# A hybrid decoder block: transfers that wait for results on GpSimd's queue, gating weights kept on chip, residual rows through shared tiles

## The chip, the cores and the metric

The kernel runs on one core of one Trainium2 chip. The metric is the time of one execution on the device in microseconds, as the median of several runs. The engines are PE (matrix products), DVE (VectorE), ACT (ScalarE), POOL (GpSimd) and SP (SyncE, which computes nothing and issues transfers between the memories). PEld is PE's loading of weights.

## The reference

One layer over 2048 tokens of width 1024. Half of the mixer is attention of eight heads of 64 with three dilated causal windows, merged by their softmax denominators; the other half is a chunked spatial gating unit. A SwiGLU network of width 2816 follows. All inputs and weights are float32.

```python
h = rms_norm(x, pre_mix_norm[l])
proj = h @ w_in[l]                       # q, k, v_a, u, v_s, 512 wide each
q = partial_rotary(q...); k = partial_rotary(k...)
attn = dilated_mixture_attention(q, k, v_a)   # (window, dilation): (128, 1), (512, 4), (2048, 16)
sgu = spatial_gating(u, v_s, ...)        # gelu(u) * (w_spatial @ layer_norm(gelu(v_s)) + b), chunks of 128
mixed = concatenate([rms_norm(attn, ...), rms_norm(sgu, ...)])
x = x + rms_norm(mixed @ w_out[l], post_mix_norm[l])
h = rms_norm(x, pre_ffn_norm[l])
f = (silu(h @ w_gate[l]) * (h @ w_up[l])) @ w_down[l]
x = x + rms_norm(f, post_ffn_norm[l])
```

## The kernel before

The tokens are cut into four blocks `m` of 512. Every float32 operand of a product is split into a high and a low part (`w_hi` and `w_lo`, `hh` and `hl`, `ah` and `al`, `ph` and `pl`), and three matmuls replace one. ACT makes the high part by a copy, DVE the low part by a subtraction.

Results travel through device memory. The projections store q, k and v (`qT`, `kT`, `vD`), the gate stores `sT`, attention stores `aT`, `out_proj` stores the residual `x1`, the feed-forward network stores `fD`. The low parts of `w_in` are stored in `wc` at their first use and read back later (`wcached`); the normalised block 0 is stored in `hD` by `ip_keep` and read back by `ip_again`. Every transfer, load or store, is issued by SP through the method `dma` (L151), so all of them stand in one queue in the order that a scheduler has fixed. An instruction of that queue that waits for a semaphore holds those behind it.

The order of the work, in `build` (L1594 on): the projections of blocks 0 and 1; then, in one merged stream, the attention of blocks 0 and 1 (`tq_heads(0)`) and the rest of the projections and gates (`w1`); then the output projections and the feed-forward network of blocks 0 and 1, merged with the attention of blocks 2 and 3 (`heads(1)`); then the output projections of blocks 2 and 3, `ffn_down(1)`, and the feed-forward network of blocks 2 and 3 with fewer products (`st_up`, `st_down`). `_merge` steps two generators in a given proportion; `R1` and `R2` set the pace of the heads.

`tq_heads` has eight steps ("banks") for each head, four of the far pattern and four of the near one. In each, `tq_scores` computes scores, a maximum and exponentials; two banks later `tq_turn` transposes them; one bank after that `pv` multiplies them with v. The loads of the next head, q, k and v together, are issued in its second bank (L1027). POOL copies q into another order there (L908, tile `q1`). `tq_merge` joins the patterns of two heads: small stores to device memory and loads from it, in three parts that later banks run.

`ip_gate` loads the spatial weights `ws` (1 MB) for each block into a slot of the ring `big` (four slots, L517), which the gate's other tiles and the inputs of the next block share.

`group` (L204) computes four PSUM banks of 128x512 over `nk` steps and calls `evac` for each bank. The projections' `evac` writes tiles of the ring `io` (four buffers) and stores them.

`out_rows` (L1178) ends `out_proj` and `ffn_down`: `evac` writes the tiles `y` (two of them), and after the last bank eight rows of 128x512 are finished by `row`: DVE adds the residual row `xs[i]`, the row is stored, and `fetch` issues the load of a later row. How many rows are loaded ahead is the buffer count of the ring that `ff_pools` names: one buffer `xr` beside `heads(1)`.

The ring `tmp` (four buffers) serves `rbw`, `araw` and `sil`. `high_priority` moves instructions forward in the scheduler's order: scores by 200 (`HP_Q`), transposes by 0 (`HP_T`).

Of the kernel before, what the change touches and what calls it, by code (L numbers as in the profile page):

```python
# [10 lines left out]
F32 = mybir.dt.float32  # L11
# [7 lines left out]
P = 128  # L19
# [64 lines left out]
SU_AT = 1  # L84
XR = 1
T_LAG = 2
T_END = 3
HP_T = 0
BIG = 3.0e38
PV_LAG = 1  # L90
GATE_LAG = 1
PV_BUF = 3
R1 = 1.2
R2 = 1.1
# [18 lines left out]
class Body:  # L113
# [32 lines left out]
    def dma(self, out, in_):  # L146
# [4 lines left out]
        self.nc.sync.dma_start(out, in_)  # L151

    def rstd(self, ss, n, inv_n, eps, name, parts=P):
        v = self.nc.vector
        a = self.tiny.tile([parts, n], F32, name=name + "_a", tag="rs_a", bufs=2, padded_shape=[P, 32])
        y = self.tiny.tile([parts, n], F32, name=name + "_y", tag="rs_y", bufs=5, padded_shape=[P, 32])
        w = self.tiny.tile([parts, n], F32, name=name + "_w", tag="rs_w", bufs=2, padded_shape=[P, 32])
        v.tensor_scalar(a, ss, inv_n, eps, ALU.mult, ALU.add)  # L158
        v.tensor_scalar(y.bitcast(I32), a.bitcast(I32), 1, None, ALU.logical_shift_right)  # L159
        v.tensor_scalar(y.bitcast(I32), y.bitcast(I32), -1, 0x5F3759DF, ALU.mult, ALU.add)  # L160
        for _ in range(3):
            v.scalar_tensor_tensor(w, y, -0.5, y, ALU.mult, ALU.mult)  # L162
            v.tensor_tensor(w, w, a, ALU.mult)  # L163
            v.scalar_tensor_tensor(y, w, 1.5, y, ALU.add, ALU.mult)  # L164
        return y

    def wtile(self, src, perm=False, shape=None, save=None, pool=None, bufs=None):
# [17 lines left out]
        if save is not None:  # L185
            self.dma(save, lo)
        return hi, lo
# [178 lines left out]
    def ip_load2(self, c, pool):  # L366
# [9 lines left out]
        def again(k):  # L376
            self.dma(self.wc[c][k], kept[k][1])
            return kept.pop(k)
# [11 lines left out]
    def ip_keep(self, m):  # L390

        for k in range(KT):
            for i in range(2):
                self.dma(self.hD[k, i], self.h[m][i][k])
                yield

    def ip_again(self, m):

        h = self.ip_tiles(m, self.ip)
        for k in range(KT):  # L400
            for i in range(2):
                self.dma(h[i][k], self.hD[k, i])
            yield
# [27 lines left out]
    def ip_kq(self, m, sec, load, tabs):  # L431
# [3 lines left out]
        def evac(b, ps):  # L435
# [13 lines left out]
            v.tensor_tensor(olv, src, ohv.bitcast(F32), ALU.subtract)  # L449
            self.dma(scr[0][b * P:(b + 1) * P, :], oh)  # L450
            self.dma(scr[1][b * P:(b + 1) * P, :], ol)

        yield from self.group(KT, load, self.feat(m), evac)

    def ip_v(self, m, load):
        nc, pool, v = self.nc, self.ip, self.nc.vector

        def evac(b, ps):
            pv = ps.rearrange("p (h e d) -> p h e d", h=4, e=2)
            for e in range(2):  # L460
                vo = pool.tile([P, 4, 2, HD], F32R, name="io", tag="io", bufs=4)
                nc.scalar.copy(vo[:, :, e, :], pv[:, :, e, :])
                v.tensor_tensor(vo[:, :, 1 - e, :], pv[:, :, e, :], vo[:, :, e, :].bitcast(F32), ALU.subtract)
                self.dma(self.vD[m][e::2, b * P:(b + 1) * P, :].rearrange("h p d -> p h d"),
                         vo.rearrange("p h s d -> p h (s d)"))
# [46 lines left out]
    def ip_gate(self, m):  # L512
# [3 lines left out]
        vh, vl, ug = part["vh"], part["vl"], part["ug"]  # L516
        ws = pool.tile([P, 2, 8, P], F32R, name="ws", tag="big", bufs=4)  # L517
        self.dma(ws, self.wsD)
        for _ in range(GATE_LAG):
# [24 lines left out]
        for ft in range(4):  # L544
# [4 lines left out]
            nc.scalar.activation(o, ps, AF.Copy, scale=self.gT[:, 12 + ft:13 + ft])  # L549
            self.dma(self.sT[m][ft], o)  # L550
            yield
# [73 lines left out]
    def to_row(self, src, dst, name):  # L625

        t = self.tiny.tile([32, 32], F32, name=name + "_w", tag="ln_w", bufs=2)
        self.nc.vector.transpose(t, src)
        self.dma(dst.rearrange("(b a) -> b a", a=32), t)

# [122 lines left out]
    def mix(self, x, h, st, pair):  # L753
# [106 lines left out]
        if h % 2 == 1:  # L860
            for mm in range(2):
# [3 lines left out]
                v.tensor_tensor(t3, t3, rb.rearrange("p (r m i) -> p r m i", r=4, m=2)[:, :, mm, :], ALU.mult)  # L865
                self.dma(self.aT[2 * x + mm][h // 2], at[:, c])
            if h == 1:
# [12 lines left out]

    def tq_pools(self, pool):
        self.ap, self.lt = pool, "at"
        self.tq = pool.tile([P, C_END - C_T4], F32, name="cstq")
        self.dma(self.tq, self.t["consts"][:, C_T4:C_END])

    def tq_load(self, x, h):
# [6 lines left out]

        qs = pool.tile([P, 4, 2, P], F32R, name="qs", tag="qs", bufs=2)
        ql = pool.tile([P, 4, 2, P], F32R, name="ql", tag="ql", bufs=2)
        ks = pool.tile([P, nkm, TB], F32R, name="ks", tag="ks", bufs=2)
# [4 lines left out]
        for m in range(nkm):  # L901
            for s in range(2):
                self.dma(ks[64 * s:64 * s + 64, m, :], rows(self.kT[m][s]))
        q1 = []
        for src in (qs, ql):
            d = pool.tile([P, 8, P], F32R, name="q1", tag="q1", bufs=2)
            for mm in range(2):
                nc.gpsimd.tensor_copy(d[:, 4 * mm:4 * mm + 4, :].rearrange("p j (r i) -> p j r i", r=4),  # L908
                                      src[:, :, mm, :].rearrange("p r (j i) -> p j r i", j=4))
            q1.append(d)  # L910
        v4 = [pool.tile([P, 4, P], F32R, name="v4", tag="v4", bufs=2 * nkm) for _ in range(nkm)]
        n0 = 0 if x == 0 else 7
        v1t = pool.tile([P, 8 * (x + 1) - n0, P], F32R, name="v1", tag="v1", bufs=2)
        for m in range(nkm):
# [3 lines left out]
            if cnt > 0:  # L918
                src = self.vD[m][h].rearrange("(j i r) d -> r i j d", r=4, i=32)
                for r in range(4):  # L920
                    self.dma(v1t[32 * r:32 * r + 32, lo - n0:lo - n0 + cnt, :], src[r, :, 4 - cnt:4])
        return qs, ql, q1, ks, v4, {n: v1t[:, n - n0, :] for n in range(n0, 8 * (x + 1))}

# [10 lines left out]
    def tq_scores(self, x, ld, units, md, h2):  # L934
# [7 lines left out]
        todo = []  # L942
        with self.tc.high_priority(HP_Q):
            for u in units:
# [68 lines left out]
    def tq_heads(self, x):  # L1013
# [6 lines left out]
        def a_step(i):  # L1020
            h, b = divmod(i, nb)
            if b == 0:
                if h == 0:
                    loads[0] = self.tq_load(x, 0)
                if h % 2 == 0:
                    stat[h // 2] = [pool.tile([P, 32], F32, name=n, tag=n, bufs=2) for n in ("tqM", "tqD")]
            if b == 1 and h + 1 < NH:  # L1027
                loads[h + 1] = self.tq_load(x, h + 1)
# [85 lines left out]
    def tq_merge(self, x, pr, stat, outs):  # L1114
# [7 lines left out]
        rr = self.dram.tile([P, 64], F32, name=f"rr{x}_{pr}")  # L1122
        self.dma(rr, T.rearrange("p s i -> p (s i)"))

        C = pool.tile([32, 2, 2, 64], F32, name="tqC", tag="tqC", bufs=1)
        rv = rr.rearrange("(q h t) e -> t q h e", h=2, t=2)
        self.dma(C[:, 1], rv[1])
        rn = rr.rearrange("(q a h t) e -> t a q h e", a=4, h=2, t=2)
        for a in range(4):
            self.dma(C[8 * a:8 * a + 8, 0], rn[0, a])  # L1130
        yield
# [14 lines left out]
        for a in range(4):  # L1146
            self.dma(ww.rearrange("t h (q a i) -> a q (t h) i", a=4, i=32)[a],
                     W[8 * a:8 * a + 8].rearrange("q t h i -> q (t h) i"))
        wb = [pool.tile([P, 4, 2, P], F32, name=n, tag=n, bufs=1) for n in ("ws", "wn")]
        for t in range(2):  # L1150
            for h2 in range(2):
                self.dma(wb[1 - t][64 * h2:64 * h2 + 64].rearrange("p r m i -> p (r m i)"),
                         ww[t, h2].partition_broadcast(64))
# [6 lines left out]
        for mm in range(2):  # L1160
            c = slice(512 * mm, 512 * mm + 512)
            v.tensor_tensor(at[:, c].rearrange("p (i r) -> p r i", r=4), un[:, :, mm, :], a1[:, :, mm, :], ALU.add)
            self.dma(self.aT[2 * x + mm][pr], at[:, c])
        if pr == 0:
# [13 lines left out]
    def out_rows(self, m, n_k, load, ops, res, gain, dst, keep):  # L1178
# [12 lines left out]
        todo = [(n, j) for n in range(2) for j in range(4)]  # L1191
        ahead = self.xr[2]

# [6 lines left out]
        def row(i, r):  # L1200
            n, j = todo[i]
            yj = y[n][:, j, :]
            v.scalar_tensor_tensor(yj, yj, r, xs[i], ALU.mult, ALU.add)
            self.dma(dst[j * P:(j + 1) * P, 512 * n:512 * n + 512], yj)
            if keep:
# [25 lines left out]
    def out_proj(self, m):  # L1231
        nc, t, v, pool = self.nc, self.t, self.nc.vector, self.fp
        ah = [self.fa.tile([P, TB], F32R, name="ah", tag="ah", bufs=KT) for _ in range(KT)]
        al = [self.fa.tile([P, TB], F32R, name="al", tag="al", bufs=KT) for _ in range(KT)]
        rb = pool.tile([P, TB], F32, name="rbw", tag="tmp", bufs=4)
        order = [4, 5, 6, 7, 0, 1, 2, 3]
        with self.tc.high_priority(HP_O):
            for kt in order:
                raw = pool.tile([P, TB], F32, name="araw", tag="tmp", bufs=4)
                if kt < 4:  # L1240
# [29 lines left out]
    def ffn_up(self, m):  # L1270
# [5 lines left out]
        for g in range(NFF // 2):  # L1276
# [17 lines left out]
            def evac(b, ps, g=g, hold=hold):  # L1294
                if b < 2:
                    s = pool.tile([P, TB], F32, name="sil", tag="tmp", bufs=4)
                    nc.scalar.activation(s, ps, AF.Silu)
                    hold[b] = s
                else:
                    s = hold[b - 2]  # L1300
                    v.tensor_tensor(s, ps, s, ALU.mult)
                    ff = 2 * g + b % 2
                    self.dma(self.fD[m][ff], s)

# [9 lines left out]
    def ffn_down(self, m):  # L1314
# [4 lines left out]
        def load_d(k, n):  # L1319
            s = pool.tile([P, TB], F32, name="araw", tag="tmp", bufs=4)  # L1320
            self.dma(s, self.fD[m][k])
# [272 lines left out]
def build(tc, t):  # L1594
    with ExitStack() as ctx:
# [35 lines left out]
        def heads(x):  # L1631
            st, pair = {}, {}
            yield from b.scores(x, 0, st)
            for h in range(NH):
# [6 lines left out]
                for _ in ahead:  # L1641
                    yield
            yield from b.attn_norm(x)

        atx = attn(0, b.tq_pools)
        G = 8 + 2 * GATE_LAG
# [4 lines left out]
                   _merge(b.ip_qkv(3), 30, b.ip_gate(3), 2 * G))  # L1651
        merge(w1, 4 * 50 + 24 + 4 * G, tq_heads(0), 133 * R1)
        atx.close()
# [5 lines left out]
        fa = fax.enter_context(tc.tile_pool(name="fa", bufs=1, side="left"))  # L1659
        b.ff_pools(ff, fa, ff, (ff, "xr", 1))  # L1660
        merge(chain(b.out_proj(0), b.out_proj(1), b.ffn_prep(0), b.ffn_up(0),
                    _merge(b.ffn_down(0), 49, b.ffn_prep(1), 12), b.ffn_up(1)), 269, heads(1), (8 * 29 + 1) * R2)
        atx.close()
        with tc.tile_pool(name="ob", bufs=1, side="right") as ob:
            b.ff_pools(ff, fa, ff, (ob, "xr", 8))
            drain(b.out_proj(2))
            b.ff_pools(ff, ob, ob, (ob, "xr", 8))
            drain(b.out_proj(3))
        fax.close()
        b.hp = ctx.enter_context(tc.tile_pool(name="hp", bufs=1, side="right"))  # L1670
        b.rw = ctx.enter_context(tc.tile_pool(name="rw", bufs=1, side="right"))
        b.ff_pools(ff, None, ff, (ff, "tmp", 4))
        with tc.tile_pool(name="pp", bufs=1, side="right") as pp:
# [37 lines left out]
```

## Time and profile before

| | |
|---|---|
| median of three runs | 2573.8 us (2573.55 to 2574.82) |
| the profiled execution, its own time | 2575.44 us |
| its span, from the first to the last instruction | 2573.7 us |
| mean granted TensorE clock | 0.958 |
| PE busy | 2328.9 us (90% of the span), 10685 matmuls |
| DVE, ACT, POOL busy | 1639.1, 1185.9 and 364.4 us |
| moved by transfers | 479.66 MB, 186 GB/s over the span |
| all of the program's transfers | queue 1, issued by SP |

Busy time counts an engine's own instructions; waiting for semaphores and issuing transfers are not counted. A granted clock of 1 is 2.4 GHz, 0.5 is 1.2 GHz; a mean lies between. A stretch in which PE is busy all the time can still be slow, if its clock is low.

### The profile page before, as it was taken

The page shows a single profiled execution, that of the slowest core. Times are in us where ns is not written, and L with a number is a line of the kernel's source. Part 1 is how long each engine was busy: PE and PEld are TensorE (multiplying, and loading weights), DVE is VectorE, ACT ScalarE, POOL GpSimd, SP SyncE. Part 2 cuts the span into 40 slices and gives each one's busy share as a digit, 9 for nine tenths or more (in the row PEclk, how much of TensorE's full clock was granted, in tenths as well). Part 3 has the DMA queues.
Part 4 walks back from the last instruction along what each step waited for, and adds up shares of the span by engine and source line. Part 5 has one row for each costly group of instructions (what it writes and reads, how often), then busy time and mean ns, then how long its engine had stood idle before and what let it go on. Part 6 is the DMA issues. An engine that isn't in the chain of part 4 may idle for free. (4 is left out here: it accounts for less than half of the span.)

```text
span 2573.7 us, 33168 instructions
## 1 busy us (share of the span) xinstructions
PE 2328.9 (90%) x10685; PEld 1890.1 (73%) x10685; DVE 1639.1 (64%) x3209; ACT 1185.9 (46%) x2278; POOL 364.4 (14%) x338
## 2 busy tenths in 40 slices
PE   7997779989869799999999999998788899999996
PEld 6776667778757678887777887777677688887774
DVE  5524354534569996768899743657677767665566
ACT  6425677556525654535555533545322233334433
POOL 0000000000000000000000000001164567641011
PEclk9998889989989899999999999999999999999998
DMA  7867666776667565456655445776465533326554
GB/s 242 296 193 237 194 201 211 244 215 204 221 207 225 156 214 155 134 154 204 201 163 186 128 123 179 213 221 205 157 214 203 200 111 103 103 86 220 173 193 167
DMA packets 350910, 479.66 MB, mean 186 GB/s; under 512 B 33264, under 2 KB 177168, under 8 KB 350224
## 3 DMA queue, kind: packets, MB, share of 16 engines
q1 hardware_dynamic: 350736, 477.55, 59.1%
q8 instruction: 84, 1.38, 0.2%
q14 instruction: 90, 0.74, 0.1%
HBM read 367.74 MB, written 109.69 MB: 186 GB/s over the span
## 5 line engine op out<-in xcount | busy, mean ns | idle before, releaser
L183 ACT CAST w_hi<-w_raw 128x512 fp32r<-128x512 f32 x368 | 226.7, 618 | 319.7 <-PE d L212 235.0
L184 DVE TENSOR_TENSOR w_lo<-w_raw,w_hi 128x512 fp32r<-128x512 f32 x368 | 255.0, 696 | 183.5 <-ACT w_hi L183 177.3
L212 PE MATMUL d<-ah,w_hi 128*128 128x512 f32 x704 | 275.1, 392 | 1.6 <-ACT ah L338 1.6
L212 PE MATMUL d<-al,w_hi 128*128 128x512 f32 x704 | 275.8, 392 | 0.0
L212 PE MATMUL d<-ah,w_lo 128*128 128x512 f32 x704 | 275.4, 391 | 0.0
L1454 PE MATMUL d<-th,w_lo 128*128 128x512 f32 x616 | 247.3, 402 | 19.5 <-DVE w_lo L1345 19.5
L1454 PE MATMUL d<-th,w_hi 128*128 128x512 f32 x616 | 244.1, 396 | 14.1 <-ACT w_hi L1344 10.1
L1454 PE MATMUL d<-tl,w_hi 128*128 128x512 f32 x616 | 244.4, 397 | 0.0
L1345 DVE TENSOR_TENSOR w_lo<-raw,w_hi 128x512 fp32r<-128x512 f32 x187 | 148.6, 828 | 91.9 <-ACT w_hi L1344 90.9
L1344 ACT CAST w_hi<-raw 128x512 fp32r<-128x512 f32 x187 | 108.4, 618 | 158.3 <-PE d L1536 108.6
L212 PE MATMUL d<-w_hi,hh 128*128 128x512 f32 x384 | 157.2, 412 | 19.6 <-ACT w_hi L201 9.6
L212 PE MATMUL d<-w_lo,hh 128*128 128x512 f32 x384 | 157.1, 409 | 5.5 <-DMA w_lo<-wc 4.9
L212 PE MATMUL d<-w_hi,hl 128*128 128x512 f32 x384 | 154.9, 405 | 0.0
L1454 PEld LDWEIGHTS d<-th,w_lo 128*128 128x128 f32 x616 | 117.9, 191 | 50.3 <-DVE w_lo L1345 25.8
L212 PEld LDWEIGHTS d<-ah,w_hi 128*128 128x128 f32 x704 | 132.1, 188 | 27.1 <-ACT ah L338 1.8
L212 PEld LDWEIGHTS d<-ah,w_lo 128*128 128x128 f32 x704 | 132.3, 188 | 26.0
L212 PEld LDWEIGHTS d<-al,w_hi 128*128 128x128 f32 x704 | 132.3, 188 | 25.7
L212 PE MATMUL d<-w_hi,fl 128*128 128x512 f32 x352 | 139.9, 405 | 11.3 <-DVE fl L1312 11.2
L212 PE MATMUL d<-w_hi,fh 128*128 128x512 f32 x352 | 143.3, 407 | 5.5 <-ACT fh L1311 5.5
L1454 PEld LDWEIGHTS d<-th,w_hi 128*128 128x128 f32 x616 | 117.9, 191 | 40.6 <-ACT w_hi L1344 10.7
L212 PE MATMUL d<-w_lo,fh 128*128 128x512 f32 x352 | 140.6, 400 | 0.0
L1454 PEld LDWEIGHTS d<-tl,w_hi 128*128 128x128 f32 x616 | 118.0, 191 | 27.1
(312 smaller groups left out, 5473.5 us busy)
## 6 DMA issues: line engine op xcount, KB each, us to landing
w_raw<-in_w_in SPq DMA_DIRECT2D x136, 256.0 KB
w_lo<-wc SPq DMA_DIRECT2D x96, 256.0 KB
w_raw<-in_w_gate SPq DMA_DIRECT2D x88, 256.0 KB
w_raw<-in_w_up SPq DMA_DIRECT2D x88, 256.0 KB
w_raw<-in_w_down SPq DMA_DIRECT2D x88, 256.0 KB
araw<-fD SPq DMA_DIRECT2D x88, 256.0 KB
raw<-fS SPq DMA_DIRECT2D x77, 256.0 KB
w_raw<-in_w_out SPq DMA_DIRECT2D x64, 256.0 KB
```

Of the source, the lines that this page charges most:

```text
L183: nc.scalar.copy(hv, rv)
L184: nc.vector.tensor_tensor(lv, rv, hv.bitcast(F32), ALU.subtract)
L212: nc.tensor.matmul(banks[b], lhsT, rhs, start=(k == 0 and j == 0), stop=(k == nk - 1 and j == len(ops) - 1))
L1344: nc.scalar.copy(hv, src)
L1345: nc.vector.tensor_tensor(lv, src, hv.bitcast(F32), ALU.subtract)
L1454: nc.tensor.matmul(ps, a[:, c], b, start=(k == 0 and n == 0), stop=(k == 3 and n == 2))
```

## The change

A method `put` issues a transfer from GpSimd's queue. The stores of results (`wc`, `hD`, `qT`, `kT`, `vD`, `sT`, `aT`, `fD`, the rows of `x1` and of the output in `out_rows`, the small ones of `to_row`), the reads of `hD` and all transfers of `tq_merge` use it. All other loads, and the transfers of `st_up` and `st_down`, stay on SP.

The gating weights `ws` are loaded once, into the pool of the first attention half, and `ip_gate` uses that tile.

`tq_load` loads q and k alone, into one buffer of q instead of two, at the sixth bank of the head before; the new `tq_near` makes the POOL copies and loads v in the first bank of the head itself. The heads of the first half get more steps (1.25 instead of 1.2), transposes get priority 200 and scores 0.

The ring `tmp` has five buffers; beside `heads(1)` the residual rows go through it, three ahead, and `xr` is gone there. In `ffn_down(1)` four of five are ahead.

```diff
-XR = 1
+T_BUF = 5
...
-HP_T = 0
+HP_T = 200
+HP_S = 0
...
-R1 = 1.2
+R0 = 1.25
...
+    def put(self, out, in_):
+        if out.dtype == F32R:
+            out = out.bitcast(F32)
+        if in_.dtype == F32R:
+            in_ = in_.bitcast(F32)
+        self.nc.gpsimd.dma_start(out, in_)
...
-            self.dma(save, lo)
+            self.put(save, lo)
...
-            self.dma(self.wc[c][k], kept[k][1])
+            self.put(self.wc[c][k], kept[k][1])
...
-                self.dma(self.hD[k, i], self.h[m][i][k])
+                self.put(self.hD[k, i], self.h[m][i][k])
...
-                self.dma(h[i][k], self.hD[k, i])
+                self.put(h[i][k], self.hD[k, i])
...
-            self.dma(scr[0][b * P:(b + 1) * P, :], oh)
-            self.dma(scr[1][b * P:(b + 1) * P, :], ol)
+            self.put(scr[0][b * P:(b + 1) * P, :], oh)
+            self.put(scr[1][b * P:(b + 1) * P, :], ol)
...
-                self.dma(self.vD[m][e::2, b * P:(b + 1) * P, :].rearrange("h p d -> p h d"),
+                self.put(self.vD[m][e::2, b * P:(b + 1) * P, :].rearrange("h p d -> p h d"),
...
-        ws = pool.tile([P, 2, 8, P], F32R, name="ws", tag="big", bufs=4)
-        self.dma(ws, self.wsD)
+        ws = self.ws
...
-            self.dma(self.sT[m][ft], o)
+            self.put(self.sT[m][ft], o)
...
-        self.dma(dst.rearrange("(b a) -> b a", a=32), t)
+        self.put(dst.rearrange("(b a) -> b a", a=32), t)
...
-                self.dma(self.aT[2 * x + mm][h // 2], at[:, c])
+                self.put(self.aT[2 * x + mm][h // 2], at[:, c])
...
-    def tq_pools(self, pool):
+    def tq_pools(self, x, pool):
...
+        if x == 0:
+            self.ws = pool.tile([P, 2, 8, P], F32R, name="wgt")
+            self.dma(self.ws, self.wsD)
...
-        qs = pool.tile([P, 4, 2, P], F32R, name="qs", tag="qs", bufs=2)
-        ql = pool.tile([P, 4, 2, P], F32R, name="ql", tag="ql", bufs=2)
+        qs = pool.tile([P, 4, 2, P], F32R, name="qs", tag="qs", bufs=1)
+        ql = pool.tile([P, 4, 2, P], F32R, name="ql", tag="ql", bufs=1)
...
-        q1 = []
-        for src in (qs, ql):
+        return [qs, ql, None, ks, None, None]
+    def tq_near(self, x, h, ld):
+        nc, pool = self.nc, self.ap
+        nkm = 2 * (x + 1)
+        ld[2] = []
+        for src in ld[:2]:
...
-            q1.append(d)
-        v4 = [pool.tile([P, 4, P], F32R, name="v4", tag="v4", bufs=2 * nkm) for _ in range(nkm)]
+            ld[2].append(d)
+        v4 = [pool.tile([P, 4, P], F32R, name="v4", tag="v4", bufs=4) for _ in range(nkm)]
...
-        v1t = pool.tile([P, 8 * (x + 1) - n0, P], F32R, name="v1", tag="v1", bufs=2)
+        v1t = pool.tile([P, 8 * (x + 1) - n0, P], F32R, name="v1", tag="v1", bufs=2 - x)
...
-        return qs, ql, q1, ks, v4, {n: v1t[:, n - n0, :] for n in range(n0, 8 * (x + 1))}
+        ld[4:] = v4, {n: v1t[:, n - n0, :] for n in range(n0, 8 * (x + 1))}
...
-        with self.tc.high_priority(HP_Q):
+        with self.tc.high_priority(HP_S):
...
+                self.tq_near(x, h, loads[h])
...
-            if b == 1 and h + 1 < NH:
+            if b == ns + 1 and h + 1 < NH:
...
-        self.dma(rr, T.rearrange("p s i -> p (s i)"))
+        self.put(rr, T.rearrange("p s i -> p (s i)"))
...
-        self.dma(C[:, 1], rv[1])
+        self.put(C[:, 1], rv[1])
...
-            self.dma(C[8 * a:8 * a + 8, 0], rn[0, a])
+            self.put(C[8 * a:8 * a + 8, 0], rn[0, a])
...
-            self.dma(ww.rearrange("t h (q a i) -> a q (t h) i", a=4, i=32)[a],
+            self.put(ww.rearrange("t h (q a i) -> a q (t h) i", a=4, i=32)[a],
...
-                self.dma(wb[1 - t][64 * h2:64 * h2 + 64].rearrange("p r m i -> p (r m i)"),
+                self.put(wb[1 - t][64 * h2:64 * h2 + 64].rearrange("p r m i -> p (r m i)"),
...
-            self.dma(self.aT[2 * x + mm][pr], at[:, c])
+            self.put(self.aT[2 * x + mm][pr], at[:, c])
...
-        ahead = self.xr[2]
+        ahead = self.xr[3]
...
-            self.dma(dst[j * P:(j + 1) * P, 512 * n:512 * n + 512], yj)
+            self.put(dst[j * P:(j + 1) * P, 512 * n:512 * n + 512], yj)
...
-        rb = pool.tile([P, TB], F32, name="rbw", tag="tmp", bufs=4)
+        rb = pool.tile([P, TB], F32, name="rbw", tag="tmp", bufs=T_BUF)
...
-                raw = pool.tile([P, TB], F32, name="araw", tag="tmp", bufs=4)
+                raw = pool.tile([P, TB], F32, name="araw", tag="tmp", bufs=T_BUF)
...
-                    s = pool.tile([P, TB], F32, name="sil", tag="tmp", bufs=4)
+                    s = pool.tile([P, TB], F32, name="sil", tag="tmp", bufs=T_BUF)
...
-                    self.dma(self.fD[m][ff], s)
+                    self.put(self.fD[m][ff], s)
...
-            s = pool.tile([P, TB], F32, name="araw", tag="tmp", bufs=4)
+            s = pool.tile([P, TB], F32, name="araw", tag="tmp", bufs=T_BUF)
...
-        atx = attn(0, b.tq_pools)
+        atx = attn(0, lambda pool: b.tq_pools(0, pool))
...
-        merge(w1, 4 * 50 + 24 + 4 * G, tq_heads(0), 133 * R1)
+        merge(w1, 4 * 50 + 24 + 4 * G, tq_heads(0), 133 * R0)
...
-        b.ff_pools(ff, fa, ff, (ff, "xr", 1))
+        b.ff_pools(ff, fa, ff, (ff, "tmp", T_BUF, 3))
...
-            b.ff_pools(ff, fa, ff, (ob, "xr", 8))
+            b.ff_pools(ff, fa, ff, (ob, "xr", 8, 8))
...
-            b.ff_pools(ff, ob, ob, (ob, "xr", 8))
+            b.ff_pools(ff, ob, ob, (ob, "xr", 8, 8))
...
-        b.ff_pools(ff, None, ff, (ff, "tmp", 4))
+        b.ff_pools(ff, None, ff, (ff, "tmp", T_BUF, T_BUF - 1))
```

## Rows read from the trace of the kernel before

**Rows 1.** Busy time by stage: stretch, its length, engines (instructions), clock, DMA share, GB/s.
```profile
core 0: us, PE busy (x) PEld busy (x) DVE busy (x) ACT busy (x) POOL busy (x), PEclk, DMA share, GB/s
0.00:186.00 186.00, 166.28 (x736) 132.31 (x736) 80.61 (x169) 87.42 (x168) 2.54 (x9) 0.99 0.75 247
186.00:380.00 194.00, 148.28 (x730) 119.25 (x729) 83.27 (x260) 116.14 (x268) 7.48 (x13) 0.87 0.69 208
380.00:712.00 332.00, 301.90 (x1547) 248.18 (x1546) 165.31 (x439) 199.93 (x439) 11.07 (x16) 0.96 0.70 220
712.00:860.00 148.00, 107.22 (x497) 87.25 (x496) 117.32 (x270) 60.06 (x123) 6.80 (x19) 0.85 0.68 208
860.00:1850.00 990.00, 945.39 (x4412) 774.70 (x4410) 722.24 (x1443) 481.44 (x848) 41.78 (x85) 0.99 0.58 174
1850.00:2574.00 724.00, 659.80 (x2772) 528.46 (x2772) 470.31 (x632) 240.94 (x434) 294.70 (x196) 0.96 0.48 162
```
**Rows 2.** Waits of PE, 186 to 860 us: total, times, longest.
```profile
PE qk L728 <- DMA ks<-kT: 21.8, 4, 12.9
PE d L212 <- DVE y L1212: 14.6, 2, 14.3
PE d L212 <- ACT w_hi L201: 9.6, 1, 9.6
PE qk L527 <- DMA ws<-wsD: 9.1, 1, 9.1
...
PE d L212 <- DVE io L449: 5.9, 4, 1.7
PE d L212 <- DMA w_lo<-wc: 4.9, 1, 4.9
```
**Rows 3.** Waits of SP's queue, 186 to 860 us: total, times, longest.
```profile
SPq L151 <- PE d L212: 86.4, 60, 5.4
SPq L151 <- ACT io L549: 21.2, 12, 6.4
...
SPq L151 <- ACT io L448: 17.3, 10, 5.8
```
**Rows 4.** Timeline of SP, 238 to 249 us: start, length, issue.
```profile
238.65 2.38 SPq L151 DMA_DIRECT2D hh<-hD  x1
...
245.85 0.62 SPq L151 DMA_DIRECT2D w_raw<-in_w_in  x1
```
**Rows 5.** Timeline of SP, 709 to 742 us.
```profile
709.01 1.29 SPq L151 DMA_DIRECT2D qs<-qT  x2
...
715.69 3.10 SPq L151 DMA_DIRECT2D vD<-io  x4
...
721.52 2.63 SPq L151 DMA_DIRECT2D vD<-io  x4
...
740.29 0.32 SPq L151 DMA_DIRECT2D araw<-aT  x1
740.66 1.83 SPq L151 DMA_DIRECT2D ks<-kT  x3
```
**Rows 6.** Instructions on tile y, 760 to 870 us: ns min/median/max, first and last start.
```profile
L1203 DVE SCALAR_TENSOR_TENSOR y<-y,po_y,xr x8: 699/746/753, 811.4 to 848.8; 128x512 f32<-128x512 f32 x8
L151 SPq DMA_DIRECT2D x<-y x8: 320/330/338, 812.1 to 849.6; - x8
```
**Rows 7.** Transfers by issue, whole span: engine, count, size of one.
```profile
fD<-sil SPq DMA_DIRECT2D x44, 256.0 KB
...
rA<-an_w SPq DMA_DIRECT2D x2, 4.0 KB
```
**Rows 8.** Groups of POOL's instructions by form, whole span: busy us, mean ns.
```profile
L1475 POOL TENSOR_TENSOR fs<-fs 128x512 f32<-128x512 f32 x11 | 19.1, 1740 | 0.0
...
L908 POOL CAST q<-qs 128x512 fp32r<-128x512 f32 x16 | 10.4, 677 | 582.6 <-issue 203.9 <-PE qk L964 198.0 <-DMA ql<-qT 179.3
```
**Rows 9.** Timeline of SP, 329 to 342 us.
```profile
336.27 5.49 SPq L151 DMA_DIRECT2D v<-vD  x8
```
**Rows 10.** The profile's costliest groups: one of the projections' three matmuls, mean ns.
```profile
L212 PE MATMUL d<-w_hi,hh 128*128 128x512 f32 x384 | 157.2, 412 | 19.6 <-ACT w_hi L201 9.6
```

## The prediction

> **What bounds the kernel now.** I read the stage windows first, because a mean over the whole span hides that the stages have different limits. PE is the busiest engine in every stage [rows 1], so time is won where PE sits idle or runs at the lower clock. Up to 186 us and after 1850 us the change touches little or nothing that PE waits for: the last stages issue their transfers as before. From 860 to 1850 us PE is idle for 990 − 945.4 = 44.6 us and its clock is 0.99, so little is to be had there. What is left is 186 to 860 us: (194 − 148.3) + (332 − 301.9) + (148 − 107.2) = 116.6 us idle, at clocks of 0.87, 0.96 and 0.85 [rows 1]. A clock of 0.87 means that a quarter of the stretch ran at 1.2 GHz. If all of these stretches had been busy, the half speed would have cost 0.13 × 194 + 0.04 × 332 + 0.15 × 148 = 61 us; much of it coincides with the idle time itself, so I call it 15 to 35 us. 116.6 + 35, some 150 us, is the ceiling of any gain in this part.
>
> Next, PE's own waits there [rows 2]: a few long ones carry it, and five name data that came late: `ks` (21.8 us in 4), `y` (14.6, of which one is 14.3), `w_hi` at L201 (9.6), `ws` (9.1), `w_lo` from `wc` (4.9). Then SP's waits [rows 3], since SP issues every load. SP is one queue in order: an issue that waits holds all behind it. It waits 86.4 us for PE to free a buffer, and 21.2 + 17.3 = 38.5 us in two rows for results that are only to be stored (`sT`, and the q and k tiles).
>
> Three SP timelines show what stands behind these waits. At 238.65 us a read of `hD` takes 2.38 us, where others take 0.38, because a buffer is not free yet; more reads follow, and only at 245.85 does the `w_raw` load go out [rows 4]; PE's 9.6 us wait for `w_hi` lies there. Between 715.69 and 724.15 us two blocks of `vD` stores sit inside the first head's q and k loads of the second attention half, and later the last `araw` load goes out only at 740.29, when a `tmp` buffer is free, with three `ks` loads behind it [rows 5]. And the eight rows of `out_proj`'s residual run from 812.1 to 849.6 us, 5.36 us apart, though each is one 0.75 us DVE instruction [rows 6]: with one `xr` buffer, load, DVE and store follow one another. PE's 14.3 us wait ends when these rows have given `y` back.
>
> **The change part by part.** *Transfers to GpSimd's queue.* By the issue counts, from `fD` (x44) to `rA` (x2), 358 transfers move [rows 7]. In 186 to 860 us POOL is busy for 7.5 + 11.1 + 6.8 us only [rows 1], so there is room. What an issue costs POOL the trace does not show. Below stands SP's 0.33 us [rows 6], above POOL's dearest instruction, 1.74 us; nearest is its copy of a 128x512 tile, 0.68 us [rows 8], since both handle one tile of that size. I take 0.7: 358 × 0.7 = 251 us spread over 1700, and even 1.74 gives 623. POOL doesn't become the bound as a whole.
>
> What it frees, wait by wait: (a) the `hD` reads leave the `w_raw` load's path, and `ws` is no longer loaded for each gate: 9.6 + 9.1 = 18.7 us of PE waiting [rows 2]. Each head's q, k and v loads stay on SP and still stand before some `w_raw` loads, so I take 12 of 18.7 (ends 0 and 18.7). (b) `w_lo` from `wc`, held up by q stores: 4.9, all of it. (c) `ks`: of 21.8 us the `vD` blocks cost 3.10 + 2.63 us and the waits around them, 8.5 us from the first to the last; a fifth `tmp` buffer lets one more load ahead. I take 9 (ends 0 and 21.8). (d) Elsewhere from 860 to 1850: 3 of 44.6 us.
>
> What is queued behind the new waits: on POOL the copies to `q1` (L908) and `k1` (L590) and the memsets at L831. The k1 copies serve a head that starts later, q1 is needed four score steps after its issue; a bank takes (712 − 186) / 64 = 8 us, so 33 us cover it. Without that cover each of the eight heads would lose a transfer's wait, some 3 us, 24 in all. The `hD` reads also wait on POOL now; behind them stand stores whose tiles have a ring of four.
>
> *That ring is the cost.* `io` has four buffers, a q or k bank takes two, and one comes back when its transfer has landed. PE already waits 5.9 us for it at L449 [rows 2]. Twelve projection groups of eight stores each: at 0.7 instead of 0.33 us a group's last store goes out 8 × 0.37 = 3 us later, 36 us in all if nothing hid it. The attention instructions that are mixed in, and the next group's first three banks, hide most: I take 8 lost (ends 0 and, at 1.74 us, 135).
>
> *Gating weights kept.* The four 1 MB loads become one, ahead of the first head's q loads: at 208 GB/s [rows 1] 1 MB takes 5 us. I take 3 lost there; the gain is in (a).
>
> *Loads of a head.* q and k now go out three score steps before use (24 us) rather than seven, v three steps before its product. Eight v loads took 5.49 us with their waits [rows 9] and two q loads 1.29 [rows 5], so a head's ten and twelve issues take some 7 and 8 us and stay hidden: 0. Cover gone, the first head loses up to 15 us, once.
>
> *Residual rows through three shared tiles.* Three loads in flight instead of one take the row chain from 37.5 us towards eight DVE instructions and one transfer, about 15 us. PE needs it only 14.3 us earlier, so all of that wait goes: 14 (ends 7, if the rows still wait behind other DVE work, and 14.6).
>
> *Priorities and pace* (transposes first, scores later, 1.25 for 1.2): the heads end some nine of 264 steps earlier, leaving nine more without attention to mix in. No row prices it: I take 0, with 10 to either side.
>
> Sum: 12 + 4.9 + 9 + 3 + 14 = 43 gained, 8 + 3 = 11 lost, and of the clock's 15 to 35 us 10 come back, as the longest idle stretches go: 42 net. The profiled execution's span 2573.7 becomes 2532. Its own time, 2575.4, is 1.7 above its span; the median of the runs is 2573.8, so by the same difference I say 2532 for the median. A change within 0.2% (5 us) can't be told from none.
>
> **The rivals.** *Nothing that matters is moved.* If the loads are late because transfers are slow, not because stores stand before them, PE waits stay. DMA shares of 0.69 and 0.70 [rows 1] speak for it, the timelines [rows 4, 5] against. Then only `y`'s 14 us come back and the 11 us of cost eat them: 2571. The Trainium skill has a rule that leads here ("DMA: Bandwidth & Descriptors", section "Issuing engines are not separate DMA queues"): several issuing engines share the same DMA engines and only save the sequencer's issue time; by it the SP time saved is no gain, as SP is not the bound. It doesn't speak of loads held behind a waiting store, which the SP timelines here show.
>
> *GpSimd's queue is slow and `io` sets the pace: slower than before.* At 1.74 us an issue the twelve groups lose 8 × 1.41 = 11.3 us each, 135 in all, and with half hidden by attention work 68. 43 + 10 − 3 gained against 68 lost: 2573.8 + 18 = 2592. It decides from about 1.4 us an issue on (half of 96 × 1.04 is 50). For it speaks that DVE is busy most of the time in 712 to 860 us [rows 1] and its two-input work shares the memory with POOL's; against it, that the next group's 96 matmuls of 0.41 us, 39 us, pass before these buffers are wanted again [rows 10]. The Trainium skill ("SBUF — State Buffer", section "Who interferes with whom") warns of this: a transfer issued by GpSimd needs descriptors that GpSimd writes, and some VectorE modes lock it out meanwhile. No run here shows it.
>
> *More comes back.* If q, k and weight loads all run ahead once SP is free, about two thirds of the 150 us ceiling goes: 2474.
>
> **How the numbers follow.** Likeliest, 2532: 0.60, its own range 2505 to 2558 (terms at their ends). More comes back: 0.16. Nothing moved: 0.08. Slower: 0.16. The range reaches into the rivals on both sides: 2480 to 2590 leaves about 2 in 10. Faster by over 0.2%: 0.60 + 0.16 = 0.76; same 0.08; slower 0.16.
>
> **What would show it.** Right: the waits of PE for `ws` and for `y` around 840 us are gone; the residual rows stand 2 us apart; the clock in 186 to 380 and 712 to 860 us is above 0.9; SP no longer waits for `io`. Wrong: POOL busy over 300 us more, PE waiting for `io` (L449, L463) tens of us, `q1` or `k1` late, or the head's first scores waiting for q, k or v.

## The result: slower by 1.2%

| kernel | median | executions | against before, 95% interval |
|---|---|---|---|
| before | 2574.3 us | 2573.6 to 2576.6 (4) | |
| after | 2606.0 us | 2598.0 to 2611.6 (4) | 1.0119 [1.0091, 1.0147] |

The forecast was 2532 us and faster, its range 2480 to 2590: wrong in sign and outside the range. The profiled execution of after took 2611.6 us, the longest of its four; its span is 2609.9.

Stages of the kernel after, in the stretches of [rows 1] (the last one is longer, as the span is):

```profile
core 0: us, PE busy (x) PEld busy (x) DVE busy (x) ACT busy (x) POOL busy (x), PEclk, DMA share, GB/s
0.00:186.00 186.00, 151.46 (x644) 119.02 (x645) 75.33 (x158) 81.06 (x156) 47.74 (x90) 0.94 0.66 226
186.00:380.00 194.00, 148.17 (x745) 120.90 (x744) 82.00 (x254) 114.37 (x258) 38.79 (x68) 0.88 0.72 213
380.00:712.00 332.00, 297.85 (x1535) 246.19 (x1536) 154.93 (x424) 204.86 (x454) 63.55 (x110) 0.94 0.65 197
712.00:860.00 148.00, 114.42 (x495) 91.06 (x494) 108.78 (x241) 59.84 (x114) 21.53 (x41) 0.87 0.73 236
860.00:1850.00 990.00, 937.65 (x4353) 769.07 (x4351) 724.50 (x1468) 476.97 (x836) 88.96 (x179) 0.97 0.57 173
```

The first stage, which the forecast left out, lost most: PE 151.5 us busy for 166.3, 644 matmuls for 736, clock 0.94 for 0.99. The stretch that was to win has the same busy time as before (148.2) and nearly the same clock (0.88 for 0.87). Followed by the starts of the same matmuls in both traces: the 65th of `d<-w_hi,hh` comes at 192.7 us for 171.2 (21.5 late); the first of `d<-ah,w_hi` at 896.6 for 879.1 (17.5); the 65th of those at 983.6 for 942.3 (41.3). The rest keeps that distance, 36 us at the end.

PE's waits of after, 186 to 860 us (total, times, longest), beside [rows 2]:

```profile
PE qk L736 <- DMA ks<-kT: 14.5, 5, 6.9
PE d L221 <- DVE io L458: 13.9, 7, 6.2
PE qk L535 <- DVE pl L1027: 11.3, 2, 11.2
PE d L221 <- ACT w_hi L192: 8.9, 2, 6.3
...
PE d L221 <- DVE io L472: 6.5, 2, 6.0
```

`ws` is gone, `y` is gone from this list, `ks` is 7 us less. But `io` takes 20.4 us (13.9 + 6.5) where it took 5.9. SP's queue in the same stretch, beside [rows 3], and the rows of `out_proj`, beside [rows 6]:

```profile
SPq L152 <- PE d L221: 220.8, 78, 49.5
SPq L152 <- ACT w_hi L210: 29.2, 33, 6.2
```

```profile
L1221 DVE SCALAR_TENSOR_TENSOR y<-y,po_y,xr x8: 734/746/752, 832.7 to 841.0; 128x512 f32<-128x512 f32 x8
L160 POOL DMA_DIRECT2D x<-y x8: 540/541/555, 835.7 to 842.0; - x8
```

SP waits no more for the engines that fill `io` (9.6 us for `vD` stores to land before v is loaded remain); it stands 220.8 us at PE's free buffers for 86.4, so loads run as far ahead as their buffers allow. The rows are 1.2 us apart for 5.36. Both came as forecast, and the kernel got slower.

Groups of POOL by form: busy us, mean ns. An issue costs 0.54 us, one of 512-byte rows (`vD`) 0.755; POOL is busy 201 us more, 565.7 in all.

```profile
L160 POOL DMA_DIRECT2D vD<-io x32 | 24.1, 755 | 73.6 <-DVE io L472 70.2 <-issue 1.7 <-DVE tqM L986 0.8
L160 POOL DMA_DIRECT2D fD<-sil x44 | 23.9, 542 | 275.4 <-DVE sil L1319 260.9 <-DVE S L754 12.5 <-PE pv L817 1.9
```

### The profile page after: what moved, and what is told of

Read it like the earlier page. It is cut to its first block, busy times and chain, and to the rows that moved or that the text cites. A ratio compares the mean times of both kernels' runs of the same rounds, so it can differ in the third digit from the quotient of the medians.

```text
span 2609.9 us, 33572 instructions
## 1 busy us (share of the span) xinstructions
PE 2342.9 (90%) x10685; PEld 1901.3 (73%) x10685; DVE 1641.8 (63%) x3209; ACT 1196.2 (46%) x2288; POOL 565.7 (22%) x696
## 5 line engine op out<-in xcount | busy, mean ns | idle before, releaser
L221 PE MATMUL d<-w_hi,hh 128*128 128x512 f32 x384 | 157.8, 413 | 28.1 <-DVE io L458 12.9
```

Source lines behind the costliest of these rows:

```text
L221: nc.tensor.matmul(banks[b], lhsT, rhs, start=(k == 0 and j == 0), stop=(k == nk - 1 and j == len(ops) - 1))
```

## The experiments

Each runs against the kernel before on the same chip; "us against before" is (ratio − 1) × 2574. A difference between two runs carries both intervals: some 10 us against e2, whose interval is the widest, 6 to 9 between most others.

### The moves against the other parts

e1 is the changed kernel with the first moved stores back on SP (first diff), e2 with all of them (second diff), e4 with the old priorities and pace (third). e3 is the kernel before with `put` in place of `dma` at the 18 places of the change, and nothing else.

```diff
-            self.put(save, lo)
+            self.dma(save, lo)
...
-            self.put(self.wc[c][k], kept[k][1])
+            self.dma(self.wc[c][k], kept[k][1])
...
-                self.put(self.hD[k, i], self.h[m][i][k])
+                self.dma(self.hD[k, i], self.h[m][i][k])
```

```diff
-        self.nc.gpsimd.dma_start(out, in_)
+        self.nc.sync.dma_start(out, in_)
```

```diff
-HP_T = 200
-HP_S = 0
+HP_T = 0
+HP_S = 200
...
-R0 = 1.25
+R0 = 1.2
```

> The changed kernel, with the stores of wc and hD back on SP's queue. Theory (early stores): on GpSimd's queue these stores leave as soon as their tiles are ready, from 19 us on, and take the transfer engines from the loads of w_raw, so ACT's copies and the normalisation behind them come late. Then PE's 7.8 us gap at 38.7 us and the half clock after it are gone, the work that stands at 193 us in the changed kernel stands near 172 us, and the time is about 2606 - 19 = 2587. Rival (order): the first 190 us are late because the other edits made the scheduler order the loads differently; then the gap stays and the time is 2600 to 2612.

> The changed kernel with every moved transfer back on SP's queue; kept gating weights, later loads of a head, pace and residual rows stay as changed. Theory (the move to GpSimd's queue is what costs, 19 us up to 193 us and some 24 us from 880 to 1040 us): the time falls to 2574 less the gains of the other parts (14 for the rows, some 9 for ws): 2550 to 2565. Rival (the loss after 880 us comes from the residual rows or the pace of the heads): only the first 19 us come back and the gains of the move are lost: 2585 to 2605.

> The kernel before with the transfers moved to GpSimd's queue and nothing else. Theory (the move costs): the early stores show as in the changed kernel, +19 us by 193 us, the later waits for w_lo and ks shrink by some 10: 2580 to 2600. Rival (the move is harmless, the other parts cost): 2555 to 2575.

> The changed kernel with the old priorities and pace: scores 200, transposes 0, 1.2 for 1.25. Theory (the move costs): within 8 us of the changed kernel, 2598 to 2612. Rival (priorities and pace upset the merged stream from 186 to 712 us): the stretch shortens by over 10 us, 2580 to 2595.

| run | median | ratio, 95% | us against before |
|---|---|---|---|
| e1 early stores on SP | 2598.7 | 1.0070 [1.0053, 1.0087] | +18 |
| e2 all on SP | 2548.8 | 0.9886 [0.9850, 0.9922] | −29 |
| e3 moves alone | 2617.8 | 1.0147 [1.0122, 1.0171] | +38 |
| e4 old pace | 2611.2 | 1.0110 [1.0089, 1.0132] | +28 |

The move to GpSimd's queue is the loss: without it the rest of the change is 29 us faster than before, 60 us from the changed kernel. e3, the moves alone, lies above the 2580 to 2600 that was expected. Pace and priorities show no part in it (e4: 2 us less than the changed kernel, within 9). The first stores carry less than the theory said, 13 us of its 19 (31 − 18), and little of it where the theory put it: PE's 7.8 us gap at 38.7 us is gone in e1, but others come in its place, and the 65th `d<-w_hi,hh` comes at 188.7 us, only 4 earlier than in the changed kernel. By the order of PE's matmuls e1 is 1 us behind the kernel before when the changed kernel stands at 50 us, and 15 behind when it stands at 150. One wait shows why. Timelines of e1, POOL and ACT:

```profile
49.68 0.73 POOL L160 DMA_DIRECT2D kT<-io  x1 [48.37 <-ACT io L457]
51.41 1.08 POOL L160 DMA_DIRECT2D kT<-io  x2 [1.00 <-DVE io L458]
```

```profile
56.49 1.02 ACT L457 CAST io<-d 128x512 fp32r<-128x512 f32 x1 [4.99 <-DMA kT<-io]
```

and the same wait in the kernel before, whose SP issued that store at 48.46:

```profile
51.44 1.08 ACT L448 CAST io<-d 128x512 fp32r<-128x512 f32 x1 [0.87 <-DMA kT<-io]
```

ACT waits for the first `io` buffer to come back: 6.8 us after its store is issued in e1, 3.0 before. That wait is of the transfer, not of the issue: the store of 49.68 us takes 0.73 us to issue and 6.7 to land.

### Which of the moves

e5 is e1 with the residual rows' stores on SP as well (first diff); e6 the changed kernel with the `io` stores on SP (second). The others go the other way, from e2, with one kind of transfer on GpSimd's queue: e7 the `io` stores (the second diff reversed), e11 the reads of `hD` (third), e12 the stores of the rows (the first reversed).

```diff
-            self.put(dst[j * P:(j + 1) * P, 512 * n:512 * n + 512], yj)
+            self.dma(dst[j * P:(j + 1) * P, 512 * n:512 * n + 512], yj)
```

```diff
-            self.put(scr[0][b * P:(b + 1) * P, :], oh)
-            self.put(scr[1][b * P:(b + 1) * P, :], ol)
+            self.dma(scr[0][b * P:(b + 1) * P, :], oh)
+            self.dma(scr[1][b * P:(b + 1) * P, :], ol)
...
-                self.put(self.vD[m][e::2, b * P:(b + 1) * P, :].rearrange("h p d -> p h d"),
+                self.dma(self.vD[m][e::2, b * P:(b + 1) * P, :].rearrange("h p d -> p h d"),
...
-            self.put(self.sT[m][ft], o)
+            self.dma(self.sT[m][ft], o)
```

```diff
-                self.dma(h[i][k], self.hD[k, i])
+                self.put(h[i][k], self.hD[k, i])
```

> The changed kernel with the stores of wc and hD and the residual rows' stores back on SP. Theory (the loss between 880 and 1040 us comes of the residual rows when their stores leave SP's queue: in the kernel with every transfer on SP it is not there, in the one with the moves alone neither): 22 us of 2598.7 come back, 2574 to 2582, and the work that stands at 942 us in the kernel before is no later against its start at 879 us than there. Rival (that loss follows from something else that was moved, as aT or fD): 2592 to 2602.

> The changed kernel with the stores from the ring io (q, k, v and sT) back on SP; all else as changed. Theory (a tile of the ring comes back later when its store shares the transfer engines with loads that SP no longer holds up; that costs some 25 us from 80 to 720 us): 2578 to 2588, PE's waits for io under 12 us. Rival (the ring costs little, the hD reads and the small stores of the merge do): 2598 to 2610.

> The changed kernel with every transfer on SP but the stores from the ring io, which stay on GpSimd's queue. Theory (ring): 2549 + 25, so 2566 to 2580, and PE waits for io some 20 us. Rival (ring costs little): 2545 to 2556.

> Every transfer on SP but the 16 reads of hD, which go out on GpSimd's queue. Theory of the prediction (these reads stood before the w_raw load that PE waited 9.6 us for): 5 to 10 us less than with all on SP, 2538 to 2545. Rival (the kept gating weights gave that wait back already, and the reads now run beside the w_raw loads): 2547 to 2556.

> Every transfer on SP but the stores of the residual rows (x1 and the rows of the output that out_rows writes), which go out on GpSimd's queue. Theory (these stores leave in bursts and hold up the loads of later rows and of xs; DVE waits for them in order, and the scores behind it): about 20 us more than with all on SP, 2564 to 2574, lost between 850 and 1000 us. Rival (they cost only together with the other moves): 2545 to 2556.

| run | median | ratio, 95% | us against before | against e2 |
|---|---|---|---|---|
| e5 | 2580.1 | 1.0022 [1.0007, 1.0037] | +6 | |
| e6 | 2614.5 | 1.0149 [1.0127, 1.0171] | +38 | |
| e7 `io` moved | 2568.7 | 0.9974 [0.9959, 0.9990] | −7 | +22 |
| e11 `hD` reads moved | 2560.1 | 0.9929 [0.9916, 0.9943] | −18 | +11 |
| e12 rows moved | 2565.3 | 0.9961 [0.9948, 0.9974] | −10 | +19 |

Each of the three kinds costs by itself, 22 + 11 + 19 = 52 of 60 us, each within some 10 us by e2's interval, so that the 11 of the `hD` reads is barely clear of none. (The stores of `wc`, `hD`, `aT` and `fD` and the merge were not tried alone.) The rows' theory holds from both sides: e5 is 12 us faster than e1, a little less than the 16 to 25 expected, and e12's loss lies where it should. Stretch from the first to the 65th `d<-ah,w_hi` in e2, after and e12:

```profile
853.00:917.00 64.00, 61.84 (x313) 50.92 (x314) 58.39 (x145) 39.81 (x74) 2.97 (x9) 0.97 0.69 210
```

```profile
897.00:984.00 87.00, 70.66 (x315) 57.25 (x314) 70.73 (x170) 46.22 (x82) 10.35 (x20) 0.82 0.52 162
```

```profile
855.00:941.00 86.00, 69.98 (x315) 56.64 (x316) 71.80 (x176) 46.93 (x82) 8.51 (x17) 0.86 0.54 165
```

The same 313 to 315 matmuls take 64 us with the stores on SP, 87 and 86 with them moved: some 14 us of idle time more, and the rest is the clock, 0.82 and 0.86 for 0.97. What starts it, in four views of e12: the timelines of SP, POOL and DVE, and PE's waits (total, times, longest).

```profile
869.01 2.25 SPq L152 DMA_DIRECT2D xr<-in_x  x3
871.36 0.86 SPq L152 DMA_DIRECT2D xs<-x  x2
872.31 0.41 SPq L152 DMA_DIRECT2D w_raw<-in_w_gate  x1
```

```profile
869.28 0.54 POOL L160 DMA_DIRECT2D x<-y  x1 [17.68 <-DVE y L1221]
870.54 2.53 POOL L160 DMA_DIRECT2D x<-y  x4 [0.72 <-DVE y L1221]
```

```profile
875.48 0.75 DVE L1221 SCALAR_TENSOR_TENSOR y<-y,po_y,xr 128x512 f32<-128x512 f32 x1 [2.11 <-DMA xr<-in_x]
```

```profile
PE qk L736 <- DVE S L744: 5.1, 1, 5.1
```

Within 4 us SP issues six loads and POOL five stores of 256 KB. The row of the last loads waits 2.11 us on DVE, the next one 0.5, in order; the scores wait behind them, and PE waits 5.1 us for the scores, from 873.4 to 878.6 us. The granted clock falls to 0.5 at 874.9 us, for 6.8 us. In e2 the same stores stand between these loads in SP's queue, and no row of this stretch waits. But the moved stores also changed the order that the scheduler fixed for DVE: in e12 the scores' instruction (L744) stands behind all eight rows, in e2 behind five. The waits for loads are 2.6 of PE's 5.1 us; how much of the stretch's 22 us is the transfers and how much the order was not separated. In e3, with one row at a time, this stretch lost 3 us: the rows three ahead and their moved stores cost only together.

The same reserve holds for every run here: an edit of a transfer makes the scheduler fix another order of the engines' work. PE's order leaves that of e2 at 52 us in e7, at 237 in e11 and at 792 in e12. A run's cost is that of the move together with the order that came with it.

e6 refutes that undoing one kind gives its cost back. In the first stage the kinds don't add: the 65th `d<-w_hi,hh` comes at 188.7 us in e1, 188.8 in e6, 189.1 in e7 and 192.7 in the changed kernel, for 169.7 in e2. Either kind is enough to lose that stage. By the order of PE's matmuls e6 is still 8 us ahead of the changed kernel at 676 us, 3 at 735, and within 2 of it from 780 to 900; between lies 740.6 us, where PE waits 12.4 us for `araw` from `sT` (12.9 in e2; the changed kernel has no such wait). Why that load is late was not followed up.

e11 refutes the forecast's term for the `hD` reads. Issued by POOL they take 6.9 us to land (median), and PE waits 5.9 us for a `w_hi` at 226.9 us; in e2 its longest wait for one from 200 to 260 us is 2.3. The time, 2560, lies above the rival's range too (2547 to 2556).

### A second queue, or GpSimd's?

The same stores from ScalarE's queue, all else as in e7 and e12:

```diff
-        self.nc.gpsimd.dma_start(out, in_)
+        self.nc.scalar.dma_start(out, in_)
```

> As the run before, but the stores from the ring io leave on the queue of ScalarE instead of GpSimd's: again a second queue, but not the one that needs GpSimd. Theory (what costs is that the stores share the engines with SP's loads): about the same, 2560 to 2585, and ACT's own waits for the low parts come on top. Rival (GpSimd's queue itself is slow): tiles come back as fast as from SP (1.7 us) and the time is 2540 to 2556.

> Every transfer on SP but the stores of the residual rows, which go out on ScalarE's queue. Theory (any second queue lets the burst of rows run beside the loads that DVE and PE wait for): near the run with these stores on GpSimd's queue, 2560 to 2572, lost between 850 and 1000 us. Rival (it is GpSimd's queue): as with all on SP, 2543 to 2555.

| run | median | ratio, 95% | us against before | against e2 |
|---|---|---|---|---|
| e8 `io` on ScalarE's queue | 2552.0 | 0.9907 [0.9889, 0.9925] | −24 | +5 |
| e13 rows on ScalarE's queue | 2571.7 | 0.9973 [0.9956, 0.9990] | −7 | +22 |

For the rows it is a second queue, whichever: 22 us against 19. For `io` it isn't: e8 can't be told from e2, and it is 17 us (within 6) faster than e7. Its time lies below the theory's range and in the rival's (2540 to 2556), though the rival's reason, tiles back as fast as from SP, doesn't hold. From issue to a store's last packet, worked out by counting the packets of each queue off against its issues (q, k, v and `sT` stores, 190 to 720 us):

| queue of the `io` stores | least | median |
|---|---|---|
| SP (e2) | 1.6 us | 2.1 us |
| ScalarE (e8) | 1.6 us | 3.1 us |
| GpSimd (e7) | 1.9 us | 3.4 us |

The least times are close; at the median a store takes 1.0 us more on the second queue, and GpSimd's adds 0.3. By the semaphores that tell of the landing the medians are 2.9, 4.2 and 4.4 us. So the tiles come back late on either queue; the first stage loses 10 us in e8 and 19 in e7. PE's wait for `io` up to 720 us in e8, beside those of the next section (the lines of its kernel are shifted by eight):

```profile
PE d L229 <- DVE io L466: 17.2, 9, 5.3
PE d L229 <- DVE io L480: 2.1, 1, 2.1
```

By the order of PE's matmuls e8 is 14 us behind e2 at the 2000th, 11 at the 3000th and 1 at the 3500th, and e7 26, 32 and 22. Some 10 us come back in both where e2 has its 12.9 us wait for `araw`, which they don't have. So late tiles cost time in e8 too while the `io` stores run, and its end hides it. What the other 17 us of e7 are stays open; 0.3 us a store doesn't explain them.

### Is it the ring?

Six `io` buffers for four in every tile of that ring, paid for with a buffer each of `ph` and `pl`; e14 is e7 with it, e15 is e2 with it.

```diff
-PV_BUF = 3
+PV_BUF = 2
...
-            oh = pool.tile([P, TB], F32R, name="io", tag="io", bufs=4)
-            ol = pool.tile([P, TB], F32R, name="io", tag="io", bufs=4)
+            oh = pool.tile([P, TB], F32R, name="io", tag="io", bufs=6)
+            ol = pool.tile([P, TB], F32R, name="io", tag="io", bufs=6)
...
```

> The stores from the ring io on GpSimd's queue, all else on SP, with six buffers in that ring in place of four (and two instead of three of ph and pl, to make room). Theory (late tiles cost time because the ring is short): the 20 us against the kernel with all on SP shrink to 0 to 8, PE's waits for io fall under 12 us. Rival (the loads that the stores delay cost the time): the distance to the run with six buffers and all on SP stays 15 to 25.

> The same six buffers of io and two of ph and pl, with every transfer on SP: the measure for the run before. Theory (ring): 2543 to 2556, PE's waits for io gain little from two more buffers here. Rival: the two buffers of ph and pl cost more than 10 us, 2560 or more, and the run before is to be read against that.

e14: 2559.0 us, 0.9925 [0.9900, 0.9950], −19 us. e15: 2551.6 us, 0.9889 [0.9868, 0.9910], −29 us. With two more buffers the moved `io` stores cost 13 us less (e14 against e7, within 8), and nothing shows with all on SP (e15 against e2, within 11). Their cost falls from 22 to 9 us. PE's wait for `io` (0 to 720 us) in e2, e7, e14, e15:

```profile
PE d L221 <- DVE io L458: 8.5, 8, 2.7
PE d L221 <- DVE io L472: 1.5, 2, 1.3
```

```profile
PE d L221 <- DVE io L458: 22.0, 12, 6.8
PE d L221 <- DVE io L472: 4.9, 3, 3.6
```

```profile
PE d L221 <- DVE io L458: 13.0, 6, 5.3
```

```profile
PE d L221 <- DVE io L458: 7.6, 6, 3.1
```

The wait is 10.0 us in e2 and 26.9 in e7; two more buffers take it to 13.0 in e14, and by the medians more than half of the cost with it: the short ring is what makes late tiles cost time, for that part. The 9 us left are hardly more than the noise.

### The other parts, with all transfers on SP

Both start from e2: e9 puts the residual rows back as before (the diff), e10 the priorities and the pace (the diff of e4).

```diff
-T_BUF = 5
+T_BUF = 4
...
-        b.ff_pools(ff, fa, ff, (ff, "tmp", T_BUF, 3))
+        b.ff_pools(ff, fa, ff, (ff, "xr", 1, 1))
...
-        b.ff_pools(ff, None, ff, (ff, "tmp", T_BUF, T_BUF - 1))
+        b.ff_pools(ff, None, ff, (ff, "tmp", T_BUF, T_BUF))
```

> Every transfer on SP, and the residual rows as in the kernel before (one buffer of their own beside the heads, ring tmp of four); kept gating weights, later loads and pace as changed. Theory of the prediction (the rows give 14 us): 2549 + 14, so 2558 to 2568. Rival (the wait for y goes, but its time is lost again in the same stretch; without the move the stretch from 706 to 853 us is as long as before): 2544 to 2555.

> Every transfer on SP, priorities and pace of the heads as in the kernel before; kept gating weights, later loads and rows as changed. Theory of the prediction (pace is worth nothing, within 10): 2545 to 2558. Rival (of the 25 us that the kernel with all on SP gains, 16 of them from 250 to 365 us, the pace carries most): 2560 to 2575.

e9: 2561.6 us, 0.9938 [0.9926, 0.9949], −16 us: the rows are worth 13 us, within 10. e10: 2541.0 us, 0.9861 [0.9847, 0.9875], −36 us: by the medians the new pace costs 7 where nothing is moved, but within 10, so that it isn't shown. e10 has the lowest median: kept weights, later loads, rows through `tmp`, one queue, old pace. The kept weights and the later loads gain 16 us with the new pace (e9), and some 23 (36 − 13) if the pace's 7 are real; they were not tried apart, since the second q buffers make the room for `ws`.

## Why the prediction was wrong

**"Up to 186 us ... the change touches little or nothing that PE waits for."** The step that failed first. The stage stores `hD`, `wc`, q, k and v, and these moved. In [rows 1] it had a DMA share of 0.75 at 247 GB/s, the highest of all, and loads that PE lives on. By the same count of packets a `w_raw` load issued from 18 to 48 us takes 2.6 us (median of 5) in the kernel before and 6.0 (of 9) after, where 26 stores leave beside them from 19.15 us on. The stretch from 18 to 48 us in before, after and e1 (columns as above):

```profile
18.00:48.00 30.00, 26.98 (x132) 20.88 (x132) 19.82 (x48) 24.37 (x50) 0.00 (x0) 1.00 0.73 249
```

```profile
18.00:48.00 30.00, 21.13 (x100) 16.64 (x101) 16.47 (x42) 22.02 (x48) 14.13 (x26) 0.90 1.02 387
```

```profile
18.00:48.00 30.00, 26.15 (x127) 20.32 (x128) 18.87 (x46) 24.00 (x49) 0.00 (x0) 1.00 0.78 254
```

The DMA engines, at a share of 0.73, are full after the move (1.02), with the stores and with more loads that SP is now free to issue; PE's first 131 matmuls stand in the same order as in e2, so PE's first long wait isn't a reordering of its own work. With these stores back on SP (e1) the load takes 2.4 us again. The stage is lost in e1 all the same, later and by the `io` ring, as it is in e7 with the `io` stores alone.

**The waiting stores hold the loads up.** The timelines [rows 4, 5] showed it truly, and with the stores gone SP runs far ahead. But loads ahead of need won nothing here, and SP's order had also kept loads back while a store went: the packets of an `io` store were done in 1.9 us (median, kernel before). The forecast saw only one of the two.

**"That ring is the cost", 8 us.** The right place, sized by the wrong quantity: the issue on POOL (0.7 taken, 0.54 measured), where the time until the tile is back decides: 22 us alone (e7), 9 with six buffers (e14 and e15). The rival of a slow GpSimd queue gave 2592 for the same wait, by an issue price of 1.74 us that doesn't exist; no issue of `kT` took over 0.54 us in the changed kernel.

**(a) `hD` reads off SP, `ws` kept: 12.** The reads cost 11 us by their move (e11, within 10). `ws` gains, with the later loads, 16 (e9) to 23 (e9 and e10), without any move. **(b), (c) `w_lo` 4.9, `ks` 9.** With all on SP PE waits 1.3 us for `w_lo` from `wc` from 186 to 860 us, and 11.0 for `ks`, less than the 14.5 after: these waits shrink without the moves.

**Residual rows, 14.** The size was right (13, e9, within 10), as long as their stores stay on SP. With these moved, rows three ahead cost 6 us (e12 against e9: −10 and −16): the loss in the stretch behind them, 24 us in the changed kernel, stood nowhere in the sum.

**Clock, 10 back.** The idle stretches only changed place: the mean clock is 0.95 for 0.958. **Pace, 0 within 10.** Held: the new pace is 2 us worse with the moves and 7 without, neither clear of the noise.

**The rivals.** *Nothing that matters is moved* was nearer to the cause than the forecast: in the first stage the transfers were the limit, once the stores left when they liked. The Trainium skill ("DMA: Bandwidth & Descriptors", section "Issuing engines are not separate DMA queues") says that issuing engines share the same DMA engines and save only issue time. The runs agree, and go further: with the `io` stores moved to either queue the median store takes 3.1 or 3.4 us for 2.1. The forecast put the rule aside for the timelines of waiting stores, and gave it 0.08. None of the rivals had the stores take the loads' bandwidth.

## What to carry to other kernels

One queue in order is also a priority: a store that holds up loads has fewer transfers beside it, and the ring that it frees comes back sooner. Before moving stores to a second queue, look at the DMA share of each stage that stores anything, and ask how long the ring can do without its tile, not what an issue costs. Try a bundle of edits without each of its parts: here 29 us of gain lay under 60 of loss.

## What the runs showed of the hardware

A 256 KB store costs POOL 0.54 us to issue, of 512-byte rows 0.755, whatever DVE does meanwhile (539 to 542 ns for all 32 of `kT`); I had bounded it by 0.33 and 1.74. Its packets are of 4096 bytes where SP's and ScalarE's are of 2048, or of 512 for `vD`. At the least the packets of an `io` store are done 1.9 us after the issue begins on POOL, and 1.6 on ScalarE and on SP.
